# Prompt attention with plain float32 matmuls on half-array tiles in place of split float32r matmuls on the whole array

## The chip, the cores and the metric

The kernel runs on one core of one Trainium2 chip. The metric is device time in microseconds (us) of one execution of the whole program. TensorE (PE) multiplies, VectorE (DVE), ScalarE (ACT) and GpSimd (POOL) do the elementwise work, and SyncE (SP) issues most of the transfers. "PEld" in a profile is the loading of a matmul's stationary operand ("weights") into the array.

## What is computed

One layer of a decoder step, all in float32: 1024 prompt tokens and 8 x 4 sample tokens go through one input projection, two mixers (a gated MLP over 128-token chunks and an attention with 8 query heads on 2 key/value heads of 64), a merge and an MLP. The change is in the attention of the prompt, which for each block of 128 queries is

```python
p_c = masked_softmax(einsum('bqkgd,bckd->bkgqc', qn, kc) * scale, m_c)   # 63 compressed keys
p_s = masked_softmax(einsum('bqkgd,bkqsd->bkgqs', qr, k_s) * scale, m_s) # selected: here all keys so far
p_w = masked_softmax(einsum('bqkgd,bskd->bkgqs', qr, k_w) * scale, m_w)  # a window of 512 keys
o = g[..., 0:1] * (p_c @ v_c) + g[..., 1:2] * (p_s @ v_s) + g[..., 2:3] * (p_w @ v_w)
```

with `g = sigmoid(gate)` per query, head and branch.

## The kernel before

**Operands.** Matmuls of the big products take `float32r` operands. To keep float32's precision each operand is split into a high part and a rest, and three products are added. In the prompt's attention the split is folded into the shapes: a key tile `KT` has the 64 rows of the high part and the 64 of the rest under each other (128 rows), a transposed query `QT` has the same query twice under each other and is itself split in two, so that a block of logits takes two matmuls over all 128 rows. A value tile `V2` has the high part and the rest side by side (64 + 64 columns), and a transposed probability tile `PH` has its high part and its rest as 256 moving columns, so that a block of PV takes one matmul of 256 columns. `V2C` and `KTC` are the same for the compressed branch.

**Units.** The prompt's attention is 32 units: 8 query blocks x 4 pairs of heads (of one key/value head). A unit has `ns = qb + 1` blocks of 128 keys in the selected branch and `nw = min(qb + 1, 5)` in the window, for each of its two heads, and one block for the compressed branch of both. These blocks stand in a row and are cut into chunks of four (512 columns, one bank of PSUM). `a_steps` computes a chunk's logits (`logits`), the negated row maxima (`stat`), exponentials with row sums (`group`), reciprocals times the gates (`fin`) and scales the probabilities on POOL (`scale`). `c_steps` is the second half, one unit later: `T` transposes a chunk on PE and splits it (ACT copies the high part, DVE subtracts), `PV` multiplies, `E` adds the two halves of the result and stores it to `o_d`. `q_load` and `q_trans` bring the queries of two units ahead from `qd_d` and transpose them.

**What runs beside it.** In the same stretch of time the compression of the sample's cache runs (tiles `hl`, `w1s`, `ch_g`, bank `F`), and blocks of the projections that nobody waits for there, called fillers here: tiles `whl` (weights) and `big` (the activations), 128x352, banks `G` and `F`, 24 matmuls per third of a block. The order of every engine's instructions is fixed when the program is built, by a scheduler with a timeline of its own; PE then takes them strictly in that order. After the prompt's attention comes the sample's attention: ten loads into `ring` (two buffers), each of 16 transfers that SP issues after reading page numbers (L924, L932), logits `S<-ring,qp`, PV `O<-ring,s_ph`. Its matmuls are plain float32 on tiles of 32 columns (`out[32 * j:32 * j + 32]`). SP issues the first `ring` transfer after the last `o_d` of the prompt's attention. Then come the rest of the fillers, the merge and the MLP, all on PE.

A plain float32 matmul stands in the trace as two weight loads and two MATMULs of the same shape; a float32r matmul and a transpose as one.

Of the kernel before, what the change touches and what calls it, by code (L numbers as in the profile page):

```python
# [37 lines left out]
PB = 8  # L38
# [7 lines left out]
def build(tc, a):  # L46
# [102 lines left out]
    KT = kvp.tile([128, 4, NP], F32R, name="KT")  # L149
    KTC = kvp.tile([128, 2, 64], F32R, name="KTC")  # L150
    V2 = kvp.tile([128, 8, 4, 2, 64], F32R, name="V2")
    V2C = kvp.tile([128, 2, 2, 2, 64], F32R, name="V2C")
# [171 lines left out]
    def kv_evac(n, ps):  # L324
        z = pq.tile([128, 512], F32, name="z", bufs=2)
        cp(z, ps, scale=rtok[:, n:n + 1])
        z3 = z[:, 0:256].rearrange("p (h d) -> p h d", d=64)
        v3 = z[:, 256:512].rearrange("p (h d) -> p h d", d=64)
        if n < 8:
            cp(V2[:, n, :, 0], v3)  # L330
            sub(V2[:, n, :, 1], v3, f(V2[:, n, :, 0]))
# [5 lines left out]
        if n < 8:  # L337
            ks = pv.tile([128, 4, 2, 64], F32R, name="ks", bufs=2)
            DVE.tensor_copy(ks[:, :, 0], z3)
            sub(ks[:, :, 1], z3, f(ks[:, :, 0]))  # L340
            ktsrc[n] = ks
        else:
            ktsrc[n] = z
            cp(vn.rearrange("p b d -> p (b d)"), z[96:128, 256:512])

    def kt_trans(n):
        src = ktsrc.pop(n)
        p = bank("O", 1)
        p4 = p.rearrange("p (h t) -> p h t", t=128)
        if n < 8:  # L350
            for h in range(4):
                PE.transpose(p4[:, h], f(src[:, h].rearrange("p a d -> p (a d)")), ident)
            cp(KT[:, :, n * 128:(n + 1) * 128], p4)
        else:
            for b in range(2):
                PE.transpose(p4[:, b], src[:, b * 128:(b + 1) * 128], ident)
            cp(knt, p4[:, 0:2, 96:128])
# [18 lines left out]
    def q_evac(n, ps):  # L376
        z = pq.tile([128, 512], F32, name="z", bufs=2)
# [9 lines left out]
        if n == 8:  # L387
            for b in range(8):
                dst = bass.AP(tensor=gs_d.tensor, offset=gs_d.offset + (b // 4) * 384 + (b % 4) * 96,
                              ap=[[3, 4], [12, 8], [1, 3]])  # L390
                SP.dma_start(dst, sgate[96 + 4 * b:100 + 4 * b, 8].rearrange("p (h c) -> p h c", c=3))
# [90 lines left out]
    def compress_prompt(which):  # L482
# [8 lines left out]
        DVE.tensor_copy(g[:, 64:128], g[:, 0:64])  # L491
        pb2 = bank("G", 1) if which == 0 else bank("O", 1)
        comp_out(pb2[:, 0:128], g, w2)
        if which == 0:
            z = comp_knorm(pb2[:, 0:128], pc, gkc, 2)
            ks = small([128, 2, 2, 64], "ckx", 1, F32R, p=pc)
            z3 = z.rearrange("p (h d) -> p h d", d=64)
            DVE.tensor_copy(ks[:, :, 0], z3)
            sub(ks[:, :, 1], z3, f(ks[:, :, 0]))
            pt = bank("F", 1)  # L500
            for kv in range(2):
                PE.transpose(pt[:, kv * 128:(kv + 1) * 128], f(ks[:, kv].rearrange("p a d -> p (a d)")), ident)
            cp(KTC, pt[:, 0:256].rearrange("p (k c) -> p k c", k=2)[:, :, 0:64])
        else:
            z3 = pb2[:, 0:128].rearrange("p (h d) -> p h d", d=64)
            POOL.memset(f(V2C), 0.0)
            for h in range(2):
                r = slice(64 * h, 64 * h + 64)
                cp(V2C[r, h, :, 0], z3[r])
                sub(V2C[r, h, :, 1], z3[r], f(V2C[r, h, :, 0]))  # L510

# [174 lines left out]
    def q_load(i):  # L686
        if i < len(pairs):
            qb, pr = pairs[i]
            qd_t[i] = p2.tile([128, 4, 2, 64], F32, name="qdl", bufs=2)
            for d in range(2):  # L690
                SP.dma_start(qd_t[i][:, :, d], qd_d[qb, :, pr * 256:(pr + 1) * 256].rearrange("p (a d) -> p a d", d=64))

    def q_trans(i):
        if i >= len(pairs):
            return
        src = qd_t.pop(i).rearrange("p a b d -> p a (b d)")
# [9 lines left out]
    def a_steps(u):  # L706

        qb, pr = pairs[u]
        kv = pr // 2
# [3 lines left out]
        runs = []  # L713
        for h in range(2):
            runs += [(h, 1, i) for i in range(ns)] + [(h, 2, i) for i in range(nw)]
        runs.append((0, 0, 0))
        chunks = [runs[i:i + 4] for i in range(0, len(runs), 4)]
        nm = small([128, 3, 6], "nm", 3, p=p2)
        sm = small([128, 3, 6], "sm", 3, p=p2)
        rs = small([128, 2, 6], "rs", 3, p=p2)  # L720
        segs, left = {}, {}
        for c, ch in enumerate(chunks):
            for i, (h, br, blk) in enumerate(ch):
                if br == 0:
                    continue
                if i and ch[i - 1][:2] == (h, br):
                    segs[h, br][-1][2] += 128
                else:
                    segs.setdefault((h, br), []).append([c, i * 128, i * 128 + 128, blk])
        for v in segs.values():  # L730
            for x in v:
                left[x[0]] = left.get(x[0], 0) + 1
        Ps, Ss, todo = {}, {}, {}

        def col(h, br):
            return 3 * h + br

        def logits(c):
            Ss[c] = bank("S", SB, psS)
            Ps[c] = p2.tile([128, 512], F32, name="P", bufs=PB)  # L740
            S = Ss[c]
            mms = []
            for (h, br), v in segs.items():
                for c_, lo, hi, blk in v:
                    if c_ == c:
                        k0 = (blk + (w0 if br == 2 else 0)) * 128
                        mms.append((h, 2 * h, lo, hi, KT[:, kv + (2 if br == 2 else 0), k0:k0 + hi - lo]))
            if chunks[c][-1][1] == 0:
                o = len(chunks[c]) * 128 - 128
                mms += [(h, 2 * h + 1, o + 64 * h, o + 64 * h + 64, KTC[:, kv]) for h in range(2)]  # L750
            first = True
# [7 lines left out]
        def stat(h, br, i):  # L759

            c, lo, hi, blk = segs[h, br][i]
            n = (hi - lo) // 128
            S = Ss[c][:, lo:hi]
            nb = ns if br == 1 else nw
            dst = nm[:, i, col(h, br):col(h, br) + 1]
            m = None
            if blk + n == nb:
# [7 lines left out]
            todo[h, br, i] = 1.0 if m is None else -1.0  # L775

        def group(h, br):
            v = segs[h, br]
            k = col(h, br)
            for i in range(1, len(v)):  # L780
                tt(nm[:, 0, k:k + 1], nm[:, 0, k:k + 1], nm[:, i, k:k + 1], OP.min)
            for i, (c, lo, hi, blk) in enumerate(v):
                ACT.activation(Ps[c][:, lo:hi], Ss[c][:, lo:hi], AF.Exp, bias=nm[:, 0, k:k + 1],  # L783
                               scale=todo[h, br, i], accum_out=sm[:, i, k:k + 1])

        def fin(ks, parts):

            n = [len(segs.get(x, "1")) for x in parts]
            for i in range(1, max(n)):
                w = [k for k, m in zip(ks, n) if m > i]  # L790
                add(sm[:, 0, w[0]:w[-1] + 1], sm[:, 0, w[0]:w[-1] + 1], sm[:, i, w[0]:w[-1] + 1])
            st = ks[1] - ks[0]
            sl = slice(ks[0], ks[1] + 1, st)
            DVE.reciprocal(rs[:, 0, sl], sm[:, 0, sl])
            mul(rs[:, 1, sl], rs[:, 0, sl], sgate[:, qb, pr * 6 + ks[0]:pr * 6 + ks[1] + 1:st])

        def scale(P, k):
            POOL.tensor_scalar(P, P, rs[:, 1, k:k + 1], 1.0, op0=OP.mult, op1=OP.mult)  # L798

        def step(c):  # L800
            logits(c)
            done = []
            for (h, br), v in segs.items():
                for i, x in enumerate(v):
                    if x[0] == c:
                        stat(h, br, i)
                        if i == len(v) - 1:
                            done.append((h, br))
            for h, br in done:
                group(h, br)  # L810
                if br == 2:
                    fin([col(h, 1), col(h, 2)], [(h, 1), (h, 2)])
                    for b2 in (1, 2):
                        for c_, lo, hi, _ in segs[h, b2]:
                            scale(Ps[c_][:, lo:hi], col(h, b2))
            if chunks[c][-1][1] == 0:
                o = len(chunks[c]) * 128 - 128
# [720 lines left out]
```

## Time and profile before

| | |
|---|---|
| median of three runs | 1849.55 us (1848.06 to 1852.17) |
| the profiled execution, its own time | 1848.68 us |
| its span, first to last instruction | 1846.9 us |
| PE busy over the span | 1761.8 us, 95% |
| DVE, ACT, POOL busy | 949.0, 703.1, 414.0 us |
| stretch of the prompt's attention (216 to 740.8 us) | 524.8 us |
| sample's attention (740.8 to 880 us) | 139.2 us |
| rest of the fillers, merge, MLP (880 us to the end) | 966.9 us |

The stretches are read off the first transposes of the queries, the first `ring` transfer and the last `O<-ring`. "Busy" is time in which an instruction of the engine stands in the record. Matmuls are pipelined, so that the record of one lasts longer than the distance to the next; where a price is wanted, the distance between the starts of like weight loads in a run is the better reading, and it is got from a merged row of the timeline as (length of the row - length of one) / (count - 1).

### The profile page before, as it was taken

The numbers are of one execution on the slowest core, as the hardware profiler recorded it, in microseconds if no ns is written. First come the engines' busy times: TensorE is split into PE (matmuls) and PEld (weight loads), VectorE is DVE, ScalarE is ACT, GpSimd is POOL, SyncE is SP. The second block draws the span as 40 slices with busy tenths as digits, with TensorE's granted clock in tenths as the row PEclk, the third lists the DMA queues.
The fourth block names the chain that finished last, engine by engine and source line by source line (L and its number), as shares of the span: only waits on it lengthen the run. The fifth ranks groups of instructions, "written<-read, shape, count | busy, mean of one in ns | idle before, by whom it ended". The sixth has DMA issues, their size and how long they took to land.

```text
span 1846.9 us, 30397 instructions
## 1 busy us (share of the span) xinstructions
PE 1761.8 (95%) x11127; PEld 1659.8 (90%) x11127; DVE 949.0 (51%) x2373; ACT 703.1 (38%) x1683; POOL 414.0 (22%) x604
## 2 busy tenths in 40 slices
PE   8999989999899999876999999999999999999999
PEld 6877889999899998523999999999999999999999
DVE  7637878777767777211765445333333333333332
ACT  5534577767667765211422332200330033003300
POOL 3103456555556655200200220000000000000000
PEclk9999989999999999987999999999999999999999
DMA  5332454333323313664553221111111111111121
GB/s 198 95 95 64 142 151 124 93 95 89 98 68 98 96 63 121 205 189 149 183 161 121 92 77 46 46 46 46 46 46 46 46 47 46 46 46 46 45 78 64
DMA packets 157992, 168.75 MB, mean 91 GB/s; under 512 B 52113, under 2 KB 132626, under 8 KB 157842
## 3 DMA queue, kind: packets, MB, share of 16 engines
q1 hardware_dynamic: 140194, 135.77, 23.9%
q0 software_dynamic: 6464, 20.19, 3.3%
q10 hardware_dynamic: 11184, 10.83, 1.8%
q8 instruction: 88, 1.44, 0.3%
q14 instruction: 62, 0.51, 0.1%
HBM read 136.56 MB, written 29.13 MB: 90 GB/s over the span
## 4 chain that ended last, share of the span: by engine, by line
PE 80%; DVE 5%; SPq 5%; DMA 3%; ACT 3%; issue 2%; POOL 1%; ACTq 0%; DVEq 0%; POOLq 0%; another core or an unknown queue 0%
PE S L73 26%; PE G L73 16%; PE PT L73 14%; PE F L73 10%; PE O L73 10%; SPq L932 3%; PE PT L844 3%; SPq L924 2%; DMA ol<-o_d 1%; ACT P L783 1%; PE PT L699 1%; DVE S L774 1%; DMA xr<-xT 0%; DVE PH L57 0%; ACT PH L54 0%
## 5 line engine op out<-in xcount | busy, mean ns | idle before, releaser
L54 ACT ACTIVATE whl<-wraw 128x1024 fp32r<-128x1024 f32 x100 | 106.1, 1061 | 411.2 <-PE S L73 144.2
L73 PE MATMUL G<-big,whl 128*128 128x352 f32 x1344 | 255.2, 333 | 2.5 <-ACT whl L54 1.5
L73 PEld LDWEIGHTS G<-big,whl 128*128 128x128 f32 x1344 | 220.6, 193 | 13.4 <-issue 5.0
L73 PE MATMUL S<-U,whl 128*128 128x352 f32 x864 | 201.6, 324 | 0.0
L73 PE MATMUL S<-H,whl 128*128 128x352 f32 x840 | 190.4, 324 | 0.0
L73 PE MATMUL PT<-U,whl 128*128 128x352 f32 x576 | 154.9, 324 | 0.0
L73 PEld LDWEIGHTS S<-U,whl 128*128 128x128 f32 x864 | 150.0, 188 | 0.0
L798 POOL TENSOR_SCALAR P<-P,rs 128x128 f32<-128x128 f32 (+4 forms) x272 | 132.8, 504 | 63.7 <-DVE rs L57 43.0
L73 PEld LDWEIGHTS S<-H,whl 128*128 128x128 f32 x840 | 144.9, 188 | 0.0
L73 PE MATMUL PT<-H,whl 128*128 128x352 f32 x528 | 143.2, 324 | 0.0
L783 ACT ACTIVATE P<-S,nm 128x512 f32<-128x512 f32 (+3 forms) x208 | 109.0, 532 | 44.1 <-DVE nm L57 32.9
L73 PE MATMUL S<-wt,big 128*128 128x512 f32 x408 | 104.1, 402 | 10.0 <-ACT wt L54 6.5
L57 DVE TENSOR_TENSOR PH<-PT,PH 128x512 fp32r<-128x512 f32 (+2 forms) x160 | 98.2, 618 | 29.6 <-ACT PH L54 28.1
L118 DVE TENSOR_TENSOR whl<-wraw,whl 128x1024 fp32r<-128x1024 f32 x80 | 97.7, 1222 | 14.6 <-ACT whl L54 14.6
L73 PEld LDWEIGHTS PT<-U,whl 128*128 128x128 f32 x576 | 103.3, 188 | 0.0
L73 PE MATMUL F<-H,whl 128*128 128x352 f32 x312 | 101.1, 324 | 0.0
L73 PE MATMUL O<-PH,V 128*128 128x256 f32 x528 | 92.1, 296 | 9.4 <-DVE PH L57 9.0
L73 PEld LDWEIGHTS S<-wt,big 128*128 128x128 f32 x408 | 76.1, 191 | 27.2 <-ACT wt L54 6.5
L54 ACT ACTIVATE PH<-PT 128x512 fp32r<-128x512 f32 (+2 forms) x160 | 86.1, 545 | 36.2 <-PE PT L844 35.3
L73 PE MATMUL O<-H,whl 128*128 128x352 f32 x312 | 99.0, 324 | 0.0
L73 PE MATMUL S<-KT,QT 128*128 128x128 f32 (+3 forms) x416 | 95.5, 340 | 2.9 <-ACT P L783 2.1
L73 PE MATMUL G<-H,whl 128*128 128x352 f32 x312 | 97.5, 324 | 0.5 <-DVE r L1373 0.5
(376 smaller groups left out, 3821.2 us busy)
## 6 DMA issues: line engine op xcount, KB each, us to landing
wraw<-wfm SPq DMA_DIRECT2D x80, 512.0 KB, 3.2
ring<-cs SPq DMA_DIRECT2D x128, 128.0 KB, 2.4
wraw<-wfm POOLq DMA_DIRECT2D x20, 512.0 KB, 3.9
tg<-th_d SPq DMA_DIRECT2D x48, 176.0 KB, 2.9
qdl<-qd_d SPq DMA_DIRECT2D x64, 128.0 KB, 2.5
raw<-cck SPq DMA_DIRECT2D x128, 64.0 KB, 1.8
raw<-ccv SPq DMA_DIRECT2D x128, 64.0 KB, 1.8
wtr<-wtok SPq DMA_DIRECT2D x24, 256.0 KB, 2.7
```

Of the source, the lines that this page charges most:

```text
L54: return ACT.activation(out, in_, AF.Copy, scale=scale)
L57: return DVE.tensor_tensor(out, x, y, op=op)
L73: return PE.matmul(out, l, r, start=start, stop=stop, skip_group_check=skip)
L118: (POOL if i < FM_BR else DVE).tensor_tensor(t[:, 1], raw, f(t[:, 0]), op=OP.subtract)
L699: PE.transpose(pt[:, j], src[:, j], ident)
L774: DVE.tensor_tensor_reduce(S, S, m, scale=-1.0, scalar=3e38, op0=OP.add, op1=OP.min, accum_out=dst)
L783: ACT.activation(Ps[c][:, lo:hi], Ss[c][:, lo:hi], AF.Exp, bias=nm[:, 0, k:k + 1], scale=todo[h, br, i], accum_out=sm[:, i, k:k + 1])
L798: POOL.tensor_scalar(P, P, rs[:, 1, k:k + 1], 1.0, op0=OP.mult, op1=OP.mult)
L844: PE.transpose(pt[:, j], Ps[c][:, j * 128:(j + 1) * 128], ident)
L924: _, vals = nc.values_load_multi_w_load_instructions(ptab[0:1, i0:i0 + 16], engines=[mybir.EngineType.SP], min_val=0, max_val=159, skip_ru ...
L932: SP.dma_start(dst, src)
```

## The change

- Keys, values, queries and probabilities of the prompt's attention stay plain float32: no high part, no rest.
- A unit is now one head of each key/value head. The weights are laid out on the host in this order (`heads`), so that the 64 rows of one head's query lie on partitions 0 to 63 and those of the other on 64 to 127, and the keys likewise. The logits of the two heads are matmuls on the upper and the lower 64 rows of the array, into two banks. PV of the two heads are matmuls on the left and the right 64 columns, into the two halves of one bank.
- The row of blocks is that of one head, so a chunk stands for both heads and has two banks `S`, two tiles `P` and two tiles `PH`.
- Each piece of a softmax is exponentiated under its own maximum as soon as its logits are there; where a branch lies in two chunks, `fin` works out the factors of the two pieces. 36 of the 96 branches do.
- `PH` is one copy, on ACT for one head and on DVE for the other. `E` is one copy.
- `z` has three buffers instead of two, and the sample's queries and outputs are rearranged with fewer copies.

```diff
-    KT = kvp.tile([128, 4, NP], F32R, name="KT")
+    KT = kvp.tile([128, 2, NP], F32, name="KT")
...
-        pt = bank("PT", 2, psS).rearrange("p (a t) -> p a t", a=4)
-        for j in range(4):
-            PE.transpose(pt[:, j], src[:, j], ident)
-        q = p2.tile([128, 2, 4, 128], F32R, name="QT", bufs=2)
-        cp(q[:, 0], pt)
-        sub(q[:, 1], pt, f(q[:, 0]))
+        pt = bank("PT", 2, psS)[:, 0:256].rearrange("p (v t) -> p v t", v=2)
+        for v in range(2):
+            PE.transpose(pt[:, v], src[:, v].rearrange("p h d -> p (h d)"), ident)
+        q = p2.tile([128, 2, 128], F32, name="QT", bufs=2)
+        cp(q, pt)
...
-            for key in sorted({m[1] for m in mms}):
-                for qi in range(2):
-                    for _, k_, lo, hi, kk in mms:
-                        if k_ == key:
-                            mm(S[:, lo:hi], q[:, qi, key], kk, first, qi == 1, True)
-                            first = False
+            for i, (v, lo, hi, kk) in enumerate(mms):
+                for h in (1, 0):
+                    r = slice(64 * h, 64 * h + 64)
+                    mm(Ss[c][h][:, lo:hi], q[r, v], kk[r], i == 0, True, True)
...
+            ACT.activation(P, S, AF.Exp, bias=dst, scale=1.0 if m is None else -1.0, accum_out=sm[:, i, k:k + 1])
+
+        def fin(br):
...
+                w = small([128, 4, 2], "fw", 3, p=p2)
+                tt(w[:, 2], nm[:, 0, sl], nm[:, 1, sl], OP.min)
+                sub(w[:, 0:2], nm[:, :, sl], w[:, 2:3].to_broadcast([128, 2, 2]))
+                ACT.activation(w[:, 0:2], w[:, 0:2], AF.Exp, scale=-1.0)
+                mul(rs[:, :, sl], sm[:, :, sl], w[:, 0:2])
+                add(w[:, 2], rs[:, 0, sl], rs[:, 1, sl])
+                DVE.reciprocal(w[:, 3], w[:, 2])
+                mul(w[:, 3], w[:, 3], gt)
+                mul(rs[:, :, sl], w[:, 0:2], w[:, 3:4].to_broadcast([128, 2, 2]))
...
-            ph = p2.tile([128, 2, 4, 128], F32R, name="PH", bufs=3)
-            cp(ph[:, 0, 0:n], pt[:, 0:n])
-            sub(ph[:, 1, 0:n], pt[:, 0:n], f(ph[:, 0, 0:n]))
-            phs[c] = ph
+            phs[c] = []
+            for h in range(2):
+                P = Ps[c][h]
+                pt = bank("PT", 2, psS).rearrange("p (a t) -> p a t", a=4)
+                ph = p2.tile([128, 4, 128], F32, name="PH", bufs=6)
...
+                cpy = DVE.tensor_copy if h else cp
+                if n - cmp_:
+                    cpy(ph[:, 0:n - cmp_], pt[:, 0:n - cmp_])
...
-                    v = V2[:, blk + (ns - nw if br == 2 else 0), kv + (2 if br == 2 else 0)]
-                    mm(O[:, h], v.rearrange("p a d -> p (a d)"), ph[:, :, j], c == 0 and j == 0, False, True)
...
+            for j, (br, blk) in enumerate(chunks[c]):
+                for h in range(2):
+                    r = slice(64 * h, 64 * h + 64)
+                    first = c == 0 and j == 0
+                    if br:
+                        mm(O[r], V[:, blk + (ns - nw if br == 2 else 0), br - 1, r], ph[h][:, j], first, False, True)
+                    else:
+                        mm(O[r], VC[:, r], ph[h][0:64, j], first, True, True)
```

The scheduler orders the new program anew. Three places of that order matter below.

**PE in the middle of the prompt's attention.** `S<-KT,QT` are logits, `PT<-ident,P` transposes of probabilities, `O<-PH` PV, `G<-big,whl` and `F<-hl,w1s` fillers and compression. Before:

```order
L73 MATMUL S<-KT,QT 128x512
L844 MATMUL PT<-ident,P 128x128 x4
L73 MATMUL S<-KT,QT 128x512
L73 MATMUL O<-PH,V_80 128x256 x4
L844 MATMUL PT<-ident,P 128x128 x4
L73 MATMUL G<-big_77,whl 128x352 x2
L73 MATMUL O<-PH,V_80 128x256 x4
L844 MATMUL PT<-ident,P 128x128 x3
```

and now:

```order
L73 MATMUL S<-KT,QT 128x512
L73 MATMUL G<-big_77,whl 128x352
L73 MATMUL O<-PH,V 64x128
L73 MATMUL G<-big_77,whl 128x352 x3
L73 MATMUL F<-hl,w1s 128x256 x2
L73 MATMUL O<-PH,V 64x128 x3
L73 MATMUL O<-PH,VC 64x128 x2
L796 MATMUL PT<-ident,P 128x128 x8
L73 MATMUL S<-KT,QT 128x512
L73 MATMUL F<-hl,w1s 128x256 x6
```

The mixture is as fine as it was, but the rows are no longer all of one shape of array: logits take 64 rows of it, `O<-PH,V` 64 columns, `O<-PH,VC` 64 rows and 64 columns, the others the whole. In the program's order of PE such a shape follows another 584 times around the prompt's attention; before, all its matmuls took the whole array. Until the last PV there are 779 fillers ahead of it on PE, where there were 1104.

**SP at the start of the prompt's attention.** `qd_d<-qz` stores a block of queries, `qdl<-qd_d` loads one for a unit. Before:

```order
L386 DMA qd_d<-qz 128x1024
L637 DMA s_d<-vs 128x4x128
L386 DMA qd_d<-qz 128x1024
L637 DMA s_d<-vs 128x4x32
L691 DMA qdl<-qd_d 128x4x64 x4
L386 DMA qd_d<-qz 128x1024 x2
```

and now:

```order
L618 DMA s_d<-vs 128x4x32
L377 DMA qd_d<-qz 128x1024 x7
L672 DMA qdl<-qd_d 128x2x64 x4
L658 DMA mask_2228<-mask 128x640
L672 DMA qdl<-qd_d 128x2x64 x2
```

The first loads now stand behind seven of the nine stores. On PE, all matmuls of the input projection (`wt`) stand ahead of the first logits, where 36 stood behind them.

**PE in the second half of the sample's attention.** `S<-ring,qp` and `O<-ring,s_ph` are its logits and PV. Before:

```order
L73 MATMUL O<-ring,s_ph 32x128 x16
L73 MATMUL S<-ring,qp 32x512 x4
L1226 MATMUL PT<-ident,s_P 128x128 x4
L73 MATMUL S<-ring,qp 32x512 x2
L73 MATMUL O<-ring,s_ph 32x128 x16
L73 MATMUL S<-ring,qp 32x512
```

and now:

```order
L73 MATMUL O<-ring,s_ph 32x128 x16
L73 MATMUL G<-big_77,whl 128x352 x21
L73 MATMUL S<-ring,qp 32x512
L73 MATMUL G<-big_77,whl 128x352
L73 MATMUL S<-ring,qp 32x512 x2
L73 MATMUL G<-big_77,whl 128x352 x20
L1174 MATMUL PT<-ident,s_P 128x128 x4
```

Fillers that stood ahead of this stage stand in it now: from the last PV of the prompt to the last matmul of the sample's attention there are 468, where there were 192, and 5953 of the program's 7200 matmuls on `whl` stand behind it, where there were 5904.

## Rows read from the trace of the kernel before

**Rows 1.** Windows: from:to length, busy of PE, PEld, DVE, ACT, POOL, clock, DMA.
```profile
216.00:740.80 524.80, 496.44 (x3513) 475.31 (x3510) 392.05 (x1276) 358.93 (x1048) 312.05 (x501) 0.98 0.35 103
740.80:880.00 139.20, 101.35 (x659) 55.92 (x660) 27.63 (x86) 26.61 (x67) 12.56 (x15) 0.84 0.58 175
880.00:1846.90 966.90, 959.81 (x5908) 957.71 (x5906) 387.33 (x682) 214.59 (x387) 31.98 (x36) 1.00 0.21 68
```
**Rows 2.** Waits, 740.8 to 880: who waited for what, us, times, longest.
```profile
PE S L73 <- DMA ring<-cs: 24.0, 17, 3.1
```
**Rows 3.** Timeline of SP, 690 to 800: the last stores, the first ring transfers.
```profile
715.28 24.12 SPq L874 DMA_DIRECT2D o_d<-o_o  x2
740.81 5.53 SPq L932 DMA_DIRECT2D ring<-cs  x8
```
**Rows 4.** PE groups by form, 216 to 740.8: count | busy, mean ns | idle before.
```profile
L73 PE MATMUL G<-big,whl 128*128 128x352 f32 x1128 | 215.0, 331 | 1.0 <-ACT whl L54 0.8
L73 PE MATMUL O<-PH,V 128*128 128x256 f32 x528 | 92.1, 296 | 9.4 <-DVE PH L57 9.0 <-DVE o_t L57 0.3
L844 PE MATMUL PT<-ident,P 128*128 128x128 f32 x560 | 90.0, 278 | 6.4 <-DVE QT L57 3.5 <-POOL P L798 1.6 <-DVE PH L57 1.2
...
L73 PE MATMUL S<-KT,QT 128*128 128x512 f32 x128 | 43.2, 417 | 1.4 <-ACT P L783 0.9 <-ACT QT L54 0.5
L73 PE MATMUL S<-KT,QT 128*128 128x384 f32 x80 | 27.1, 380 | 0.0
L73 PE MATMUL S<-KT,QT 128*128 128x128 f32 x112 | 22.6, 250 | 1.5 <-ACT P L783 1.2 <-DVE QT L57 0.3
L699 PE MATMUL PT<-ident,qdl 128*128 128x128 f32 x128 | 20.4, 284 | 2.2 <-DVE PH L57 2.2
L73 PE MATMUL S<-KTC,QT 128*128 128x64 f32 x128 | 19.9, 259 | 1.3 <-ACT P L783 1.3
L73 PE MATMUL S<-KT,QT 128*128 128x256 f32 x96 | 19.9, 308 | 0.0
```
**Rows 5.** Timeline of weight loads: start, length, rows*columns of the weights, count.
```profile
207.05 5.51 PEld L73 LDWEIGHTS F<-wt,big 128*128 128x128 f32 x24
...
772.07 0.19 PEld L73 LDWEIGHTS G<-big,whl 128*128 128x128 f32 x1 [0.84 <-issue]
772.43 0.81 PEld L73 LDWEIGHTS O<-ring,s_ph 128*32 128x32 f32 x32 [0.17 <-issue]
...
112.70 1.86 PEld L73 LDWEIGHTS F<-c,cw 128*128 128x128 f32 x16
...
304.59 0.54 PEld L73 LDWEIGHTS O<-PH,V 128*128 128x128 f32 x4
...
305.19 0.46 PEld L844 LDWEIGHTS PT<-ident,P 128*128 128x128 f32 x4
...
306.08 0.53 PEld L73 LDWEIGHTS S<-KTC,QT 128*128 128x128 f32 x4
306.53 2.23 PEld L73 LDWEIGHTS G<-big,whl 128*128 128x128 f32 x14
```
**Rows 6.** Timeline of PE, 770.9 to 774: start, length, rows*columns, moving shape, count.
```profile
770.68 0.48 PE L73 MATMUL G<-big,whl 128*128 128x352 f32 x2
771.10 1.04 PE L73 MATMUL S<-ring,qp 128*32 128x512 f32 x2
772.07 0.42 PE L73 MATMUL G<-big,whl 128*128 128x352 f32 x1
772.43 1.08 PE L73 MATMUL O<-ring,s_ph 128*32 128x128 f32 x32
```
**Rows 7.** Timeline of PE, 111.9 to 113.2: weights on 24 rows between full ones.
```profile
111.72 0.40 PE L73 MATMUL S<-wt,big 128*128 128x512 f32 x1
112.04 0.73 PE L373 MATMUL O<-ident,gt 24*128 24x24 f32 x9
112.70 0.71 PE L73 MATMUL F<-c,cw 128*128 128x128 f32 x4
```

More of the change, by code (lines that the diff above doesn't have):

```diff
@@ L336, in kv_evac @@
         SP.dma_start(a["kvo"][n], z)
[L337 to L343, printed above, removed]
+        ktsrc[n] = z
+        if n == 8:
             cp(vn.rearrange("p b d -> p (b d)"), z[96:128, 256:512])
@@ L495, in compress_prompt @@
             z = comp_knorm(pb2[:, 0:128], pc, gkc, 2)
[L496 to L499, printed above, removed]
             pt = bank("F", 1)
-            for kv in range(2):
-                PE.transpose(pt[:, kv * 128:(kv + 1) * 128], f(ks[:, kv].rearrange("p a d -> p (a d)")), ident)
-            cp(KTC, pt[:, 0:256].rearrange("p (k c) -> p k c", k=2)[:, :, 0:64])
-        else:
[L505 to L510, printed above, removed]
+            PE.transpose(pt[:, 0:128], z, ident)
+            cp(KTC, pt[:, 0:64])
+        else:
+            cp(VC, pb2[0:64, 0:128])
     evac_next()
@@ L712, in a_steps @@
         w0 = ns - nw
[L713 to L716, printed above, removed]
+        runs = [(1, i) for i in range(ns)] + [(2, i) for i in range(nw)] + [(0, 0)]
         chunks = [runs[i:i + 4] for i in range(0, len(runs), 4)]
[L718 to L719 removed]
+        nm = small([128, 2, 6], "nm", 3, p=p2)
+        sm = small([128, 2, 6], "sm", 3, p=p2)
         rs = small([128, 2, 6], "rs", 3, p=p2)
[L721 removed]
+        segs = {}
         for c, ch in enumerate(chunks):
[L723 to L727, printed above, removed]
[L728 to L736 removed]
+            for i, (br, blk) in enumerate(ch):
+                if i and ch[i - 1][0] == br:
+                    segs[br][-1][2] += 128
+                else:
+                    segs.setdefault(br, []).append([c, i * 128, i * 128 + (128 if br else 64), blk])
+        Ps, Ss = {}, {}
         def logits(c):
[L739 to L741 removed]
+            Ss[c] = [bank("S", SB, psS) for _ in range(2)]
+            Ps[c] = [p2.tile([128, 512], F32, name="P", bufs=PB) for _ in range(2)]
             mms = []
[L743 removed]
+            for br, v in segs.items():
                 for c_, lo, hi, blk in v:
@@ L786, in fin @@
[L786 to L795, printed above, removed]
@@ L829, in a_steps @@
+            for br, v in segs.items():
+                if v[-1][0] == c:
+                    fin(br)
         return chunks, Ps, [lambda c=c: step(c) for c in range(len(chunks))]
@@ L871, in E @@
+        def E():
             o = small([128, 128], "o_o", 2, p=p2)
-            for h in range(2):
-                POOL.tensor_tensor(o[64 * h:64 * h + 64], t1[0:64, h], t3[:, h], op=OP.add)
+            cp(o, O_[0])
             SP.dma_start(o_d[4 + pr, :, qb * 128:(qb + 1) * 128], o)
@@ L1184, in fin_group @@
         ots.append(ot)
-        for h in range(8):
-            kv, gg = divmod(h, 4)
-            r0 = kv * 16 + gg * 4
-            dst = ot[(gg % 2) * 64:(gg % 2) * 64 + 64, 2 * kv + gg // 2]
-            DVE.tensor_copy(dst.rearrange("p (j t) -> p j t", t=4), O4[kv * 64:kv * 64 + 64, :, r0:r0 + 4])
+        for kv in range(2):
+            rows = slice(kv * 64, (kv + 1) * 64)
+            DVE.tensor_copy(ot[rows].rearrange("p g (j t) -> p g j t", t=4),
+                            O4[rows, :, kv * 16:kv * 16 + 16].rearrange("p j (g t) -> p g j t", t=4))
     done = None
@@ L1424, in layout @@
     w = d["w_in"][0]
-    wu, wv, wq = w[:, 0:512], w[:, 512:1024], w[:, 1024:1536]
+    heads = np.array([4 * kv + g for g in range(4) for kv in range(2)])
+    wu, wv = w[:, 0:512], w[:, 512:1024]
+    wq = w[:, 1024:1536].reshape(1024, 8, 64)[:, heads].reshape(1024, 512)
+    wbr = d["w_branch"][0]
+    wbr = np.concatenate([wbr[0:512], wbr[512:].reshape(8, 64, 1024)[heads].reshape(512, 1024)], 0)
     wkc, wvc = w[:, 1536:1664], w[:, 1664:1792]
```

154 lines of the change are left out of this document (61 added, 93 removed).

## The prediction

> **What bounds the kernel now.** I read the windows first, cut at the first transposes of the queries, the first `ring` transfer and the last matmul of the sample's attention [rows 1]. In the first stretch PE is busy for 496.4 of 524.8 us while DVE has 392, ACT 359 and POOL 312: PE sets its length, and PE is full because fillers stand between the attention's steps. The third stretch is PE alone, 959.8 of 966.9 us. Only in the second does PE wait: 101.4 of 139.2 us busy, at a mean clock of 0.84, and the largest single wait is for `ring` transfers, 24.0 us [rows 2]. SP can't issue them sooner, because the last two stores of the prompt's attention hold its queue until 740.8 us [rows 3]. So the time is PE's work plus PE's waits (28.4 + 37.9 + 7.1 us in the three stretches), the end of the prompt's attention starts the second stretch, and what DVE, ACT and POOL save counts only where PE waits for them.
>
> **Prices on PE.** From runs of weight loads of one shape, (length of the run - one load) / (count - 1), with 0.19 us for one load, 0.14 for a transpose's [rows 5]: float32r with 512 columns 0.231 us, with 352 (a filler) 0.157, with 256 (PV) 0.117, with 64 columns 0.113, which is the pace of the loads themselves; a transpose 0.107. Plain float32, `F<-c,cw` with 128 columns: 0.111 for each of its two instructions; I take it in proportion to the columns, 0.44 for 512. Two such instructions with 512 columns stand in 1.04 us, first load and last latency included, which fits [rows 6].
>
> **The attention's matmuls, before.** Logits [rows 4]: 128 x 0.231 + 80 x 0.172 (384 columns, between 352 and 512) + 96 x 0.117 + (112 + 128) x 0.113 = 82 us. PV: 528 and two per unit for `V2C`, 592 x 0.117 = 69. Transposes: 688 x 0.107 = 74. Sum 225.
>
> **After.** The program has 264 logit matmuls, two heads to a pair: pairs of 512, 384, 256, 128 and 64 columns are 36, 16, 24, 24 and 32. If the two heads run side by side, a pair takes two slots, 0.89, 0.67, 0.44, 0.22 and (by the load) 0.22 us: 32 + 10.7 + 10.7 + 5.3 + 7 = 66 us. One after the other it is 132. PV has 592 matmuls, a pair in two slots of 0.111: 66 us; 656 transposes: 70. Sum 202, so 23 us less. That halves of the array work side by side is seen for columns: 32 instructions of `O<-ring`, on four tiles of 32 columns, take 1.08 us all in all [rows 6], 0.034 each, where one on the whole array takes 0.111. No row shows two tiles of rows. I take side by side, since the nearest row has it, and 202 to 268 as the bounds. By the Trainium skill ("TensorE: Matmul & The Clock Gate", Part 3: Packing small matmuls) tiles of rows overlap as well, four of them measured at 3.07 times one; by it the sum is the 202.
>
> **The change of shape.** This is the term that decides. In a run of one shape the next weights are loaded while the matmul ahead still streams: loads of fillers follow each other at 0.157 us though each MATMUL is recorded with over 0.3. Where the shape of the array changes they are not: the filler at 770.68 ends at 771.16, and the two `S<-ring` end at 772.14, 0.98 us later, where 0.89 is their own, so 0.09 us more; the next filler ends 0.35 us after them, 0.19 more than its 0.157; the 32 `O<-ring` end 1.02 us later, 0.13 more than eight slots of 0.111; and the load of that run starts at 772.43, 0.06 before the matmul ahead has ended [rows 5, 6]. A tile of 24 rows does the same: after it four `F<-c,cw` take 0.64 us for 0.44 of work, 0.20 more [rows 7]. So a change costs 0.09 to 0.20 us, nearly all where 128 columns of weights must be loaded behind it. The new order has 584 changes: 142 into the 64-row logits, which load 128 columns (0.19), 190 into PV with 64 columns (0.15, between 0.13 and 0.19), 143 back into full matmuls (0.19), 109 back into transposes (0.15, their load being shorter): 27 + 28.5 + 27 + 16.4 = 99 us. All at 0.09 it is 53, all at 0.20 it is 117. The rows show it for tiles of 24 rows and 32 columns, none for 64. The Trainium skill ("TensorEngine Tiling (Array Packing)", Key Properties) says that changing the tiling mode drains the engine, whatever the size; by it the 99 stands, and without it for tiles of 64 the time is that of the first rival.
>
> **Fillers.** By the order, about 800 instead of 1128 [rows 4] are done when the prompt's last store lets SP go on (779 ahead of the last PV, and some 20 until the store, as before): 328 x 0.157 = 51 us leave the first stretch. Of these 276 (43 us) come into the second and 49 (8 us) behind it.
>
> **Waits in the first stretch.** Before 28 us, of them 9.0 for DVE's subtraction for `PH` [rows 4]. `PH` is one copy now instead of a copy and a subtraction, and PE, being later, finds more done: I leave 6. Against that, the first loads of queries wait for seven stores instead of two, and no projection matmuls are left to fill the first units: 10 us. So 16, bounds 8 to 40; the upper one also stands for the two banks that a chunk now takes out of three `S` banks. The nine small steps of `fin` for a split branch (36 times) lie on DVE and ACT, which lose more than that with the subtractions, and a unit ahead of PE's need; the cover is the slack of 130 us that DVE has in this stretch. More stores for the gates stand early, ahead of nothing that waits.
>
> **The sum.** First stretch 496 - 23 + 99 - 51 + 16 = 537 against 525: +12. Fewer transposes of keys (16 for 32) ahead of it: -2. Second stretch: 101.4 + 43 = 144 us of PE work in 139 us; with PE fed, its clock should stay up (0.84 to 1.00 is 16 us of its 101), and some waits for `ring` remain; I take 145, so +6, bounds 0 (SP's issue alone sets it) and +20. Behind it +8. In all +24: 1848.7 + 24 = **1873 us** of a profiled execution. The median before, 1849.55, lies 0.9 above the profiled run, which changes nothing. Its own range, by the bounds of switches (-46, +18), waits (-8, +24) and second stretch (-6, +14), not all at one end: 1828 to 1908.
>
> **Rivals.**
> - *The change of shape costs nothing for tiles of 64* (faster). For: no row of such a tile. Against: 24 rows and 32 columns both pay. Then the first stretch loses 99 us, PE is no longer late and the 28 us of waits stay (+12): 1786. It decides below about 0.13 us a change (75 us in all), where the 24 us are gone.
> - *Cheap changes under waits* (faster or none). 0.09 a change as at 771.16 [rows 6], and each falls where PE would wait anyhow: -46 and -10, so about 1817 to 1850. Against: four of the five readings are higher.
> - *The two heads don't run side by side in logits* (the change doesn't do what it says). For: no row of it. Logits then cost 66 us more: 1939.
>
> **How the numbers follow.** Forecast 0.66, first rival 0.13, second 0.13, third 0.08. A measurement here can tell about 0.2% (4 us) from no change. Faster by that: the first rival, 0.10 of the second, and 0.01 of the forecast's tail, 0.24; within it 0.04; slower 0.72. The range 1815 to 1925 leaves out the first rival and most of the third, 0.2 in all.
>
> **What would show it.** Right: loads of the first `S<-KT`, `O<-PH` or filler behind another shape that start only at the end of the matmul ahead, a filler behind an attention step at 0.35 us instead of 0.157; the two heads' MATMULs starting within a few ns; the first `ring` transfer near 750 us; PE waits well under 38 us and a clock near 1.0 in the sample's attention. Wrong: a first `ring` transfer before 720 us (changes of shape are cheap), or logit pairs that start 0.9 us apart (no overlap); PE waits over 40 us in the first stretch would mean that another engine or the `S` banks set it.

## The result, and the profile after

The changed kernel takes 1926.1 us (median, 1925.0 to 1929.0) against 1848.8 us: 1.042 times the time before, 95% interval 1.040 to 1.045. Slower was forecast, but by 24 us; it is 77 us. The profiled execution has a span of 1923.2 us, 76.3 more than before.

The three stretches of the changed kernel, cut as in [rows 1] (from:to, length, busy time and instructions of PE, PEld, DVE, ACT, POOL, granted clock, share of the DMA engines, GB/s):

```profile
229.40:788.30 558.90, 549.35 (x3662) 401.13 (x3661) 316.41 (x1166) 291.73 (x946) 247.51 (x398) 0.97 0.27 78
788.30:938.30 150.00, 135.02 (x941) 94.70 (x940) 29.47 (x85) 35.50 (x80) 33.81 (x36) 0.99 0.61 190
938.30:1923.20 984.90, 971.89 (x5962) 970.06 (x5962) 391.01 (x682) 216.91 (x393) 33.92 (x38) 0.99 0.20 67
```

The start of the attention moved from 216.0 to 229.4 us mostly because some 60 projection matmuls (14 us) that stood in the first stretch stand ahead of it now. Its end is what counts: the first `ring` transfer left SP at 788.3 us instead of 740.8, 47.5 later. The second stretch is 10.8 us longer, the third 18.0. DVE, ACT and POOL do less than before, and PE waits less: 9.6 us in the first stretch for 28.4, 15.0 in the second for 37.9. So the loss is PE's own work. What PE still waited for in the first stretch (waits: who for what, us, times, longest); its waits for `PH` come to 0.3 us in the groups below, against the 9.0 in [rows 4]:

```profile
PE PT L796 <- DVE fw L757: 2.7, 1, 2.7
PE S L73 <- ACT P L740: 2.2, 2, 1.9
PE S L73 <- ACT QT L54: 1.5, 2, 1.0
```

and in the second, against the 24.0 us of [rows 2]:

```profile
PE S L73 <- DMA ring<-cs: 8.8, 9, 1.8
```

And the groups of PE by shape in the first stretch (line, names, weights rows*columns, moving shape, count | busy us, mean ns | idle before), which answer to [rows 4]:

```profile
L73 PE MATMUL G<-big,whl 128*128 128x352 f32 x792 | 166.5, 341 | 1.1 <-ACT whl L54 1.1
L73 PE MATMUL O<-PH,V 128*64 128x128 f32 x1056 | 104.4, 286 | 0.3 <-ACT PH L54 0.3
L796 PE MATMUL PT<-ident,P 128*128 128x128 f32 x528 | 90.3, 285 | 3.0 <-DVE fw L757 2.7 <-ACT PH L54 0.3
L73 PE MATMUL S<-KT,QT 64*128 64x512 f32 x144 | 72.9, 661 | 0.0
L73 PE MATMUL S<-KT,QT 64*128 64x256 f32 x96 | 28.5, 413 | 0.3 <-ACT P L740 0.3
L73 PE MATMUL S<-KT,QT 64*128 64x384 f32 x64 | 28.1, 534 | 0.0
```

A "busy" of a group counts a moment once, also where two matmuls run in it. The 144 instructions of 512 columns are 36 pairs; had each pair been side by side, 1.13 us as in the pair shown below, they would fill 41 us. They fill 72.9.

**Where PE's time went.** For this table each matmul is charged with the time from the latest end recorded ahead of it to its own end, less the wait ahead of it; the charges and the waits of a run add up to its span, but for some 4 us behind the last matmul. Times in us, over the whole execution; `pairs_h`, `whole` and `before_h` are runs of the next section.

| | before | after | pairs_h | whole | before_h |
|---|---|---|---|---|---|
| logits of the prompt | 81.2 | 132.7 | 92.2 | 130.8 | 83.3 |
| PV of the prompt | 75.9 | 109.8 | 87.4 | 142.7 | 78.1 |
| transposes of queries and probabilities | 81.4 | 90.8 | 95.5 | 79.1 | 83.1 |
| compression | 55.3 | 69.0 | 62.3 | 56.8 | 55.2 |
| the 7200 matmuls on `whl` | 1179.3 | 1196.1 | 1187.6 | 1182.3 | 1185.2 |
| projection, sample's attention, rest | 291.3 | 276.3 | 276.7 | 278.9 | 275.4 |
| waits of PE | 78.4 | 44.4 | 57.6 | 54.4 | 66.5 |
| first `ring` transfer at | 740.8 | 788.3 | 738.5 | 756.6 | 705.2 |

Logits cost 51.5 us more where the prediction had 11 (16 less for the matmuls, 27 more for their changes of shape). That is the greater part of the miss.

**The heads apart.** Two places of the changed kernel, the timeline of PE (start, length, names, shapes, count). First a lone head:

```profile
483.78 0.27 PE L73 MATMUL O<-PH,V 128*64 128x128 f32 x1
483.98 0.75 PE L73 MATMUL G<-big,whl 128*128 128x352 f32 x3
484.66 1.12 PE L73 MATMUL S<-KT,QT 64*128 64x512 f32 x2
485.71 0.66 PE L796 MATMUL PT<-ident,P 128*128 128x128 f32 x4
```

and here a pair:

```profile
416.67 0.60 PE L796 MATMUL PT<-ident,P 128*128 128x128 f32 x4
417.20 1.13 PE L73 MATMUL S<-KT,QT 64*128 64x512 f32 x4
418.26 0.43 PE L73 MATMUL O<-PH,V 128*64 128x128 f32 x2
```

Two instructions (one head) take 1.12 us, four (both heads) 1.13. So halves of rows do run side by side, the second at no extra time; and a head that stands alone pays the price of two. In the trace 41 groups of logits are one head's 512 columns alone, 1.05 us each from the end of the work ahead, and 9 are a pair, 1.06 in eight of them. The order that stands ahead of the prediction shows it too: there each `S<-KT,QT 128x512` stands by itself, with a filler or a matmul of the compression behind it. Counted over that whole order, the half that streams longer in each group of logits has 57,728 columns, where pairs throughout would give 35,840; for PV 46,208 of 75,776 instead of half. At 0.222 us for 128 columns (two instructions of 0.111) that is 38 us more for logits and 14 for PV. PV also stands split (one head's two instructions, 0.36 us, in 61 places).

**The changes of shape.** The same rows give their price again. The lone head ends 1.05 us after the filler ahead (484.73 to 485.78), where its two instructions have 0.86 to 0.89 of work; the three fillers end 0.68 after the PV ahead (484.05 to 484.73), where 3 x 0.157 is 0.47. And the weights come late, as in [rows 5] and [rows 6]; timeline of the loads at the lone head:

```profile
483.98 0.46 PEld L73 LDWEIGHTS G<-big,whl 128*128 128x128 f32 x3 [0.17 <-issue]
484.66 0.29 PEld L73 LDWEIGHTS S<-KT,QT 64*128 64x128 f32 x2 [0.22 <-issue]
485.71 0.42 PEld L796 LDWEIGHTS PT<-ident,P 128*128 128x128 f32 x4 [0.76 <-issue]
```

Each starts 0.07 us before the matmul ahead ends, whatever it is. All 584 changes of the order stand in the trace. In 578 of them PE did not wait, and their time from end to end beyond the pace of the shape adds up to 100 us, 0.173 each. The medians go by what follows: 0.14 us for PV, 0.15 for a transpose, 0.18 for logits, 0.20 for a full matmul.

### The profile page after: what moved, and what is told of

It reads as the page before. It is cut to its first block, busy times and chain, and to the rows that moved or that the text cites. A ratio compares the mean times of both kernels' runs of the same rounds, so it can differ in the third digit from the quotient of the medians.

```text
span 1923.2 us, 31142 instructions
## 1 busy us (share of the span) xinstructions
PE 1873.4 (97%) x11654; PEld 1647.0 (86%) x11654; DVE 880.1 (46%) x2259; ACT 648.8 (34%) x1606; POOL 377.8 (20%) x531
## 4 chain that ended last, share of the span: by engine, by line
PE 89%; SPq 3%; DMA 3%; DVE 2%; issue 1%; ACT 1%; POOL 0%; ACTq 0%; DVEq 0%
PE S L73 30%; PE G L73 17%; PE PT L73 13%; PE O L73 12%; PE F L73 12%; PE PT L796 4%; SPq L881 2%; SPq L873 1%; DMA ol<-o_d 1%; DMA ring<-cw 1%; DMA ring<-cs 1%; PE PT L681 0%; DMA xr<-xT 0%; PE PT L798 0%; ACT ou L54 0%
## 5 line engine op out<-in xcount | busy, mean ns | idle before, releaser
L73 PE MATMUL G<-big,whl 128*128 128x352 f32 x1344 | 268.4, 339 | 9.0 <-ACT whl L54 7.2
L740 ACT ACTIVATE P<-S,nm 128x512 f32<-128x512 f32 (+4 forms) x264 | 126.2, 483 | 113.2 <-DVE nm L739 88.5
L764 POOL TENSOR_SCALAR P<-P,rs 128x512 f32<-128x512 f32 (+4 forms) x264 | 128.6, 503 | 153.0 <-DVE rs L57 112.3
L73 PE MATMUL S<-KT,QT 64*128 64x512 f32 (+3 forms) x400 | 129.1, 501 | 3.8 <-ACT P L740 2.2
L739 DVE CUSTOM_DVE_ANT_0 S<-S,mask 128x512 f32<-128x512 f32 (+3 forms) x160 | 76.9, 497 | 79.4 <-PE S L73 74.3
L73 PE MATMUL O<-PH,V 128*64 128x128 f32 x1056 | 104.4, 286 | 0.3 <-ACT PH L54 0.3
L73 PEld LDWEIGHTS O<-PH,V 128*64 128x64 f32 x1056 | 67.8, 137 | 32.4 <-issue 21.4
```

Of the source, the lines that this page charges most:

```text
L73: return PE.matmul(out, l, r, start=start, stop=stop, skip_group_check=skip)
L739: DVE.tensor_tensor_reduce(S, S, m, scale=-1.0, scalar=3e38, op0=OP.add, op1=OP.min, accum_out=dst)
L740: ACT.activation(P, S, AF.Exp, bias=dst, scale=1.0 if m is None else -1.0, accum_out=sm[:, i, k:k + 1])
L764: POOL.tensor_scalar(P, P, rs[:, i, k:k + 1], 1.0, op0=OP.mult, op1=OP.mult)
```

## Experiments

All times are medians beside runs of the kernel before on the same chip (1845.6 to 1848.5 us). A ratio is to the kernel before, with its 95% interval.

**The heads kept together.** In `pairs_h` the order is held by added dependencies; the arithmetic stays. `behind(a, b)` lets `a` wait for `b`; `free_S` holds the exponentials of the head that is done first, `lastcp` the copy of a chunk's second `PH`; the last condition puts the fillers from the 34th third of a block on behind the last PV.

```diff
+                    m_ = mm(Ss[c][h][:, lo:hi], q[r, v], kk[r], i == 0, True, True)
+                    if i == 0 and h == 1 and free_S:
+                        behind(m_, free_S[-1])
...
+                    if j == 0 and h == 0:
+                        behind(m_, lastcp[c])
...
+                    if k == 0 and b * 3 + c == 33:
+                        tc.add_manual_dep(m_.ins, last_pv[0].ins.name, ...)
```

> The changed kernel with two added orderings and one cap: the first logit matmul of a chunk waits until the exponential of the chunk before has freed a bank for each head, the first PV matmul waits for both PH copies, and fillers beyond 33 thirds of a block stand behind the last PV (779 stand ahead of it in the changed kernel, 792 here). In the order the two heads then stand together: the columns that one of the two halves must stream, in plain float32, fall from 96 to 64 us for logits and from 77 to 66 us for PV, and the changes of the array's shape from 588 to 380. Theory 1 (my failed step was that I counted the heads as running side by side where the order keeps them apart; the changes cost 0.175 us each, as the changed kernel's trace has it): -43 us for the heads, -36 us for the changes, so about 1847 us against 1926. Theory 2 (the heads were side by side already or gain nothing by it, only the changes cost): -36, about 1890. Theory 3 (a waiting head was hidden under waits of PE, which come back now): less than 15 us gained, above 1911.

Measured: 1869.0 us (1865.3 to 1871.8), ratio 1.012 [1.010, 1.014]; 57 us less than the changed kernel. The groups of logits and PV in its first stretch:

```profile
L73 PE MATMUL O<-PH,V 128*64 128x128 f32 x1056 | 81.6, 284 | 2.3 <-DVE PH L812 1.3 <-DVE fw L57 1.0
L73 PE MATMUL S<-KT,QT 64*128 64x512 f32 x144 | 47.6, 677 | 2.1 <-ACT P L747 2.1
L73 PE MATMUL S<-KT,QT 64*128 64x256 f32 x96 | 15.7, 413 | 0.0
L73 PE MATMUL S<-KT,QT 64*128 64x384 f32 x64 | 14.7, 537 | 0.2 <-ACT P L747 0.2
```

The same 144 instructions with 512 columns, each as long as before by itself (677 ns for 661), fill 47.6 us instead of 72.9. By the table logits fall by 40.5 us and PV by 22.4; all work of PE falls by 73, close to the 79 of theory 1, and part of that are the changes, 380 for 588 in the order. Of that 13 us come back as waits, as a pair must wait until two banks are free:

```profile
PE S L73 <- ACT P L747: 12.8, 8, 3.9
```

So theory 1 holds for the work, and its time was 22 us too low, 13 of them for those waits and 6 for work that did not go; some 3 stay open. The hold on the fillers was not run alone on the changed kernel; it puts 792 instead of 779 of them ahead of the last PV, 2 us of work.

**Only the logits together.** `pairs_lh` leaves out the line on `lastcp`.

> Of the three edits of pairs_h only two: the two heads' logits kept together and the fillers held at 792; PV is ordered as the scheduler likes. By the order the columns to stream fall from 96 to 64 us for logits and stay at 77 us for PV, changes of shape fall from 588 to 485. Theory 1 (my failed step is the logits' heads standing apart, at the price of a lone half): -32 - 18 = -50, so about 1876 us, most of what pairs_h gained (1926 to 1869). Theory 2 (the gain of pairs_h came from PV, or from holding the fillers): not below 1900.

Measured: 1886.0 us (1884.8 to 1892.2), ratio 1.021 [1.018, 1.024]: 40 us of the 57. Logits are charged with 91.2 us as in `pairs_h`, PV with 109.6 as in the changed kernel. The greater part is the logits, as theory 1 has it, 10 us short of its 50.

**No halves of rows; no halves at all.** In `whole_l` the queries carry 64 rows of zeros, so that each head's logits are a matmul over all 128 rows with the keys of both; in `whole` PV also takes all 128 columns of `V`, of which half is used.

```diff
+        POOL.memset(q[64:128, :, 0], 0.0)
+        POOL.memset(q[0:64, :, 1], 0.0)
+        cp(q[0:64, :, 0], pt[0:64])
+        cp(q[64:128, :, 1], pt[64:128])
...
+                    mm(Ss[c][h][:, lo:hi], q[:, v, h], kk, i == 0, True, True)
...
+                        mm(O[:, h], V[:, blk + (ns - nw if br == 2 else 0), br - 1], ph[h][:, j], first, False, True)
```

> The changed kernel with only the logits on all 128 rows (zeros in the other head's rows of the queries), PV on halves as it is. Changes of shape fall from 588 to 363, columns of the logits rise from 96 to 119.5 us, PV stays (78 for 77). Theory 1 (0.175 us a change): -39 + 24 = -15, about 1911 us. Theory 2 (changes cost nothing in the end): +24, about 1950.

Measured: 1898.2 us (1897.0 to 1900.0), ratio 1.028 [1.026, 1.030].

> The changed kernel without tiles of half the array: queries stand with 64 rows of zeros (a memset and a copy for each head), so that logits take all 128 rows, and PV takes all 128 columns of V into a place of its own for each head, of which half is used. Nothing runs side by side any more, and in the order the changes of shape fall from 588 to 83. The columns to stream rise from 96 to 119.5 us for logits and from 77 to 126 us for PV: +72 us. Theory 1 (a change costs 0.175 us in the end-to-end time): 505 fewer, -88 us, so about 1910 us. Theory 2 (the drains seen at changes lie under waits, or the next matmul catches up): +72 us, about 1998.

Measured: 1932.3 us (1930.9 to 1934.3), ratio 1.046 [1.045, 1.048]. Both are far from theory 2 (1950 and 1998). `whole` streams 72 us more than the changed kernel and takes 6 us more; by the table logits cost what they cost on halves (130.8 for 132.7) although each streams alone, and transposes, compression and fillers, whose matmuls are the same, lose 38 us between them, which goes with the 83 changes that are left of 588. (The 72 are the expectation's count, at 0.213 us for 128 columns; at the measured 0.222 they are 75.) Theory 1 missed by 22 us in `whole`: 10 are waits, some 3 are that pace; the rest I can't assign. In `whole_l` it missed by 13 the other way, 4 of them waits.

**Logits whole, PV in pairs.** `mix_h` joins `whole_l`, the PV of `pairs_h` and the hold on the fillers.

> The changed kernel with the logits on all 128 rows (as in whole_l), PV on halves with the two heads kept together (as in pairs_h) and 792 fillers ahead of the last PV. Changes of shape 226, against 363 in whole_l and 380 in pairs_h; columns to stream 119.5 us for logits, 65 for PV. Theory 1 (columns of the longer half, plus 0.175 us a change): whole_l's 1898 less 13 for PV's columns and 24 for 137 changes, about 1861 us, so no worse than pairs_h (1869), although its logits stream twice the time. Theory 2 (what helped in pairs_h is work side by side): about 1885 or more.

Measured: 1874.8 us (1872.3 to 1877.4), ratio 1.016 [1.013, 1.018]. It lies between the two, and 14 us above theory 1. With 226 changes for 380, and logits charged with 135.0 us for 92.2, it is 6 us slower than `pairs_h`, which the two intervals do not tell from none: what the pairs of rows save, their changes of shape nearly eat.

**The price of a change, by itself.** In the MLP, where PE is busy from end to end, 224 matmuls are made plain float32, as two halves of 64 columns in `halves_mlp` and undivided (one slice of 128) in `whole_mlp`:

```diff
+                if halves and c == 0 and not first:
+                    for r in (slice(0, 64), slice(64, 128)):
+                        mm(pss[c][r, 0:TB], f(w[:, 0, k + woff, r]), f(src[:, 0, k, c * TB:(c + 1) * TB]), False, False, True)
+                    continue
```

> The kernel before, where the same 224 matmuls of the MLP as in halves_mlp are plain float32 on the whole array. From the pace of 0.111 us for 128 columns of one of two instructions, 352 columns take 0.61 us for 0.157: +102 us, about 1950 us. All theories say the same; it is the base that halves_mlp is read against.

> The kernel before, where in each of the 32 first-layer blocks of the MLP seven of the 192 matmuls (those of the high parts, first third, but the first k) are plain float32 in two halves of 64 columns, each writing its 64 rows of the bank; the result is the same. 224 pairs, 448 changes of shape, in a stretch in which PE is busy from end to end. To be read against whole_mlp, which has the same matmuls undivided. Theory 1 (halves run side by side, each change costs 0.15 to 0.20 us of the end-to-end time): whole_mlp plus 448 x 0.175 = 78 us. Theory 2 (the drain is made up for by the matmuls behind): within 10 us of whole_mlp. Theory 3 (halves run one after the other): whole_mlp plus 224 x 0.61 = 137 us and more.

Measured: 1942.0 us for `whole_mlp` (ratio 1.050 [1.048, 1.053]) and 2019.2 for `halves_mlp` (1.092 [1.089, 1.095]). The difference is 77.2 us (73 to 81, with two executions of each), 0.172 us for each of the 448 changes: theory 1, and a price of the whole execution, not of a record. Half of these changes lead into 64 columns and half into full matmuls; the medians of the changed kernel's trace for these, 0.14 and 0.20, have the mean 0.17. Timeline of PE, first undivided, then in halves:

```profile
1302.46 0.33 PE L73 MATMUL S<-H,whl 128*128 128x352 f32 x1
1302.63 0.92 PE L73 MATMUL PT<-H,whl 128*128 128x352 f32 x3
1303.39 0.33 PE L73 MATMUL S<-H,whl 128*128 128x352 f32 x1
```
```profile
1321.96 0.32 PE L73 MATMUL S<-H,whl 128*128 128x352 f32 x1
1322.21 1.17 PE L73 MATMUL PT<-H,whl 128*64 128x352 f32 x5
1323.22 0.32 PE L73 MATMUL S<-H,whl 128*128 128x352 f32 x1
```

From one `S<-H` to the next it is 0.93 us undivided and 1.26 in halves, with the same columns: two changes, 0.33 us. `whole_mlp` itself came 8 us below its forecast: 0.417 us more for a matmul instead of 0.454.

**Fewer fillers in the attention, on the kernel before.** The profile after suggested it: with some 280 fillers more in the sample's attention PE waited there 15.0 us instead of 37.9, and the clock was 0.99 instead of 0.84. `before_h` is the kernel before with the hold of `pairs_h` alone.

> The kernel before with one cap: fillers beyond 33 thirds of a block stand behind the last PV of the prompt's attention, so 792 stand ahead of it for 1104, and the 312 others come into the sample's attention. Theory A (PE's waits of 36 us and its low clock of 0.84 in the sample's attention are for want of work there): the first stretch gets 49 us shorter, the second takes 49 us more of matmuls but loses some 20 us of waits and some 15 us of slow clock, so about 1815 us against 1849. Theory B (the attention of the prompt is bound by the chain of its own steps, and fillers there cost nothing): the first stretch stays at 525 us with more waits, and the second gets longer, about 1849 or more.

Measured: 1830.7 us (1828.5 to 1833.6), ratio 0.991 [0.989, 0.993]: 0.9% faster than the kernel before, and faster than the changed one. With the same hold the paired halves of `pairs_h` take 1869.0: on equal terms the change, even in pairs, costs 38 us. The first two stretches of `before_h`:

```profile
216.30:705.10 488.80, 453.23 (x3199) 430.17 (x3198) 377.33 (x1251) 346.46 (x1023) 288.75 (x479) 0.98 0.35 102
705.10:859.30 154.20, 138.04 (x969) 97.26 (x967) 42.94 (x108) 35.82 (x89) 31.82 (x35) 0.97 0.60 185
```

Against [rows 1] the attention is 36 us shorter, not 49, as PE waits 35.6 us in it for 28.4; the second stretch is 15 us longer with 37 us more of matmuls in it. Theory A, at somewhat under half its gain.

> The kernel before with the fillers held at 40 thirds of a block (960) instead of 33 (792). With 33 the time fell from 1846 to 1831: PE lost 21 us of waits and 16 us of slow clock in the sample's attention, and won 8 us of waits, 10 us of slower fillers and steps elsewhere. Theory A (what the sample's attention needs is some 250 fillers, so fewer can be held back): about 1825, waits of PE in the prompt's attention back from 37 to about 32 us. Theory B (each filler held back gains alike): 144 held for 312, half of the gain, about 1839.

> The kernel before with the fillers held at 26 thirds of a block (624 ahead of the last PV; 1104 in the kernel before, 960 gave 1848 us, 792 gave 1831). Of the 168 more that are held some pass behind the sample's attention, which had 464 of them with 792. Theory A (the sample's attention had what it needs with 792): the first stretch gets some 25 us shorter less 10 us of new waits, and the work comes back later, about 1830. Theory B (the prompt's attention still loses by its fillers): about 1815.

Measured: 1848.4 us with 40 thirds (ratio 1.000 [0.998, 1.001]) and 1844.1 with 26 (0.998 [0.997, 1.000]). No theory had that. The stretches (two of 40 thirds, then the last two of 26):

```profile
215.20:729.20 514.00, 480.10 (x3372) 456.83 (x3371) 387.38 (x1267) 354.41 (x1042) 302.04 (x491) 0.97 0.35 102
729.20:873.50 144.30, 114.82 (x794) 70.88 (x792) 35.14 (x92) 28.73 (x70) 21.07 (x24) 0.93 0.59 181
```
```profile
679.20:837.80 158.60, 140.37 (x979) 97.87 (x977) 47.89 (x115) 37.72 (x91) 36.07 (x37) 0.97 0.60 189
837.80:1845.20 1007.40, 994.59 (x6106) 991.85 (x6105) 400.98 (x703) 223.44 (x403) 41.42 (x48) 1.00 0.20 67
```

With 40 the sample's attention has 135 matmuls more than before and still 29.5 us of waits: too little to feed it, while the waits of the first stretch (33.9) are up already. With 26 it has no more matmuls than with 33 (979 for 969), the rest passes behind it, where it costs its full price. So the gain lies near 33; where its best point is, and why the first 144 fillers held back gave nothing, these runs don't settle.

## Why the prediction failed

**What held.** PE is the bound, and its waits shrank. The changes of shape: 99 us forecast for 584, 100 in the trace and 0.172 us each end to end in the MLP, against 0.09 to 0.20 as bounds; the prices by kind (0.15 for PV and transposes, 0.19 for logits and full matmuls) came within 0.01 of the medians. This is the drain that the Trainium skill names ("TensorEngine Tiling (Array Packing)", Key Properties); it gives no size, and the runs do. The fillers: 792 ran before the first `ring` transfer where some 800 were forecast. Waits in the first stretch were 9.6 us for the 16 I took, within 8 to 40. In the sample's attention they fell to 15.0, at a clock of 0.99. Halves of rows run side by side (1.13 us for a pair, 1.12 for one), as I chose without a row for it.

**What failed.** The step "264 logit matmuls, two heads to a pair ... 66 us": I asked whether the array can run two heads side by side, and not whether the order puts them there. The order took each head's matmuls apart; a chunk needs two of the three `S` banks, and a dependency on what frees the second (`pairs_lh`, `pairs_h`) brought them together. That the scheduler goes by the bank that comes free is an inference from this. Logits were charged with 40 us more than the steps add up to, PV with 8 more; the columns that stream with no partner are worth 38 and 14. The end of the first stretch came 37.5 us later than forecast (788.3 for 750.8), and the 48 us are more than all of it, the waits having come out 6 us lower; what makes up for the remaining 5 is not assigned. `pairs_lh` and `pairs_h` give 40 and 57 us back with the order alone, fewer changes (485 and 380 for 588) being part of that. From the table's 333.3 us for logits, PV and transposes, the changes into them at the prediction's prices (142 x 0.19 + 190 x 0.15 + 109 x 0.15 = 72) leave 261; this way of charging had 238.5 for the kernel before where the prediction's sum was 225, so about 248 stand against the bounds of 202 to 268. They held, but I took the lower end by the nearest row, where the program that I had before me would have told the place between them.

**The third rival** had this place and the wrong cause. It priced all heads alone, 66 us more, 1939 us; what came is three fifths of that (40 of 66). The time of 1926 is nearer to it than to the forecast, yet the array does what the change says.

**The rest of the miss**, 15 us, lies in the other two stretches. The sample's attention took 150 us for 145 forecast, inside the bounds. Behind it 18 us came instead of 8: 54 more matmuls (8.8 us at 0.163), 6 us more of waits, and about 3 of matmuls at a lower clock behind them, which the granted clock of two places shows (0.50 and 0.51, the lower of its two levels):

```profile
963.00:966.40 3.40, 3.40 (x13) 3.40 (x13) 3.03 (x6) 0.50 (x1) 1.13 (x3) 0.50 0.39 112
993.70:1000.60 6.90, 4.22 (x15) 4.08 (x15) 2.67 (x6) 0.50 (x1) 0.00 (x0) 0.51 0.59 179
```

The first as a timeline of PE:

```profile
954.54 4.05 PE L73 MATMUL F<-big,whl 128*128 128x352 f32 x24
962.78 5.65 PE L73 MATMUL G<-big,whl 128*128 128x352 f32 x24 [4.19 <-ACT whl L54]
```

After a wait of 4.19 us for weights 24 fillers take 5.65 us instead of 4.05.

**A term I left out.** The attention's first 50 us run at a granted clock of 0.76, before at 0.90 (windows of after, the second of them the part at the lower level; then of before):

```profile
225.00:275.00 50.00, 45.96 (x256) 35.71 (x254) 27.02 (x122) 25.97 (x93) 22.74 (x41) 0.76 0.56 157
232.60:256.40 23.80, 21.15 (x95) 16.10 (x95) 11.28 (x67) 12.65 (x51) 11.31 (x25) 0.50 0.64 187
```
```profile
225.00:275.00 50.00, 44.38 (x283) 40.46 (x282) 36.84 (x160) 36.29 (x124) 28.57 (x57) 0.90 0.50 148
```

That is some 7 us (0.14 of 50), and it lies within the charges of the table. There the first units' steps wait for each other (1.03 us ahead of the first logits at 231.7), and no filler stands on PE before 249.6; the 10 us that I had put on this start as waits came as clock and waits together.

## What to carry to other kernels

Work that shares the array saves time only where the two halves stand next to each other in the engine's order: before pricing them side by side, count in the program how many do, and tie them together (here one dependency each) if the scheduler sees them as separate. Price every change into and out of plain float32 tiles of half the array at 0.14 to 0.20 us of TensorE time, by what follows, and count the ways back as well as the ways in; with some five matmuls from one change to the next (2,750 around 584) this ate the gain of the halves. A stage that waits for transfers is the place for work that nobody waits for, but only in the amount that fills it.

## What was not expected of the hardware

- Which side is halved ahead, rows, columns or both, makes no difference to a change: in each of the 578 changes without a wait the next weight load starts 0.06 to 0.07 us before the end of the matmul ahead. What follows does: 0.14 us into 64 columns of weights, 0.15 into a transpose, 0.18 to 0.20 into 128 columns (medians); 0.173 on the mean, and 0.172 in the MLP.
- A transpose with 64 columns of weights is no such change. In these rows of the changed kernel it ends 0.11 us after the full one ahead (503.61 to 503.72), the pace of full ones, and the logits behind it pay as they do behind any full matmul:

```profile
503.23 0.38 PE L796 MATMUL PT<-ident,P 128*128 128x128 f32 x2
503.45 0.27 PE L798 MATMUL PT<-ident,P 128*64 128x128 f32 x1
503.65 1.12 PE L73 MATMUL S<-KT,QT 64*128 64x512 f32 x2
```

- Not every small tile pays. In the kernel before, float32r matmuls with 24 columns of weights stand among full matmuls, and neither way shows a price. Behind one of them four transposes take 0.44 us (100.36 to 100.80), and behind these two such matmuls take 0.32 (to 101.12), the pace of full ones:

```profile
100.04 0.32 PE L73 MATMUL F<-big,wg 128*24 128x352 f32 x1
100.20 0.60 PE L352 MATMUL O<-ident,ks 128*128 128x128 f32 x4
100.56 0.56 PE L73 MATMUL PT<-big,wg 128*24 128x352 f32 x2
```

- Whether a float32r matmul on half of the columns pays for a change was not tried.
